# Hybrid encoder on one core: attention probabilities stored head-outermost, GpSimd writing the meta tokens' copies, and a weight split held behind the last merges

## The chip, the cores and the metric

The kernel runs as one program on one core of a Trainium2 chip. The metric is the device time of one execution in microseconds (us); the engines are PE (TensorE), DVE (VectorE), ACT (ScalarE), POOL (GpSimd) and SP (SyncE, which issues most DMAs). A matmul appears in the profile twice, as a weight load (PEld) and as the matmul itself (PE).

## The reference

Two encoder layers over 272 tokens (16 learned meta tokens and 256 real ones), 2048 channels, float32. Each layer:

```
h = rmsnorm(x);  q,k,v,f,ga,gf = h @ w_in
q,k = rope(rmsnorm(q)), rope(rmsnorm(k))
attn = softmax(q k^T / sqrt(128)) v          # 8 query heads, 2 kv heads
a = attn @ w_attn_br;  s = Re(fft2(f)) @ w_four
x = x + (sigmoid(ga)*a + sigmoid(gf)*s) @ w_out
x = x + (silu(dwconv3(rmsnorm(x) @ w_up_gate)) * (rmsnorm(x) @ w_up_val)) @ w_down
```

The meta tokens are dropped from the output, so the second layer computes its queries from token 14 on (`lo = 14`, 258 columns) where the first computes all 272 (`lo = 0`).

## The kernel before

Weights stream from HBM in chunks of 512 KB. Every chunk `raw` is split into a high part `wh` (ACT, line 303, a cast to fp32r) and a low part `wl` (DVE, line 306, the difference, two inputs in SBUF). A product is then three fp32r matmuls (lines 375 to 377): high by high, high by low, low by high. The activations stand split in the same way (`xH`/`xL`, `mH`/`mL`). Splits run up to three chunks ahead of PE (`LOOK = 3`); `split_w` issues them from a list, between pairs of matmuls.

Other work is put between the weight matmuls of the branch stage: a helper is a generator, each `yield n` waits for n pairs of matmuls, and `step()` advances it. The attention is such a generator. It runs beside the gate projections `ga` and `gf`, for one kv head (four query heads) at a time. Per kv head there are nine items: one for the meta tokens' queries of all heads, and for each of four heads two blocks of 128 queries. An item goes through

- `scores`: three matmuls into `ps_s`, maximum `mx` and bias `nb` on DVE, exponential on ACT (line 1079) into `pn`, one of four buffers of 128 queries by 384 columns; columns 112 to 383 hold the 272 probabilities, the meta tokens first; an ACT copy (line 1080) puts the 16 meta columns at 0, 32 and 64 too;
- `normalise`: reciprocal `rs` on DVE (line 1085), and one POOL instruction that scales all 384 columns of `pn` (line 1086);
- `transposed`, two items later: three PE transposes into `ps_pt`, then `PH`, the high part, on ACT (line 1106), `PL` and the meta rows' low part on DVE (lines 1107, 1109);
- `values`, for a head whose two blocks were transposed: seven matmuls into `ps_pv` (lines 1116 to 1119), three for each of two key blocks and one for the meta block.

`PH` is stored as (block, head, token) with 3 blocks and 4 heads, `PL` as (block, head, token) with 2. The program's order between engines is kept by semaphores that the framework sets from the regions that instructions read and write; it also orders each engine's instructions by a schedule of its own, except where code asks for the written order (`keep_in_program_order`).

At the end of each half of the branch stage come the merges: for each of the last channels, two DVE instructions make `th`, ACT casts `mH` (line 1227) and DVE makes `mL` (line 1228). The output projection `ps_o` (line 376 reads `mL`) follows at once.

Of the kernel before, what the change touches and what calls it, by code (L numbers as in the profile page):

```python
# [10 lines left out]
F32 = mybir.dt.float32  # L11
F32R = mybir.dt.float32r
AF = mybir.ActivationFunctionType
ALU = mybir.AluOpType
AX = mybir.AxisListType

P = 128
D = 2048
NM = 16
SEQ = 256  # L20
T = NM + SEQ
# [132 lines left out]
def _rep(ap, n):  # L154
    return ap.unsqueeze(1).to_broadcast([ap.shape[0], n, ap.shape[1]])
# [23 lines left out]
def encoder_kernel(ctx, tc, xT, params, consts, bmat, cfold, csign, w_fl, w_f64c, w_in, w_abr, w_four, w_f64, w_out, w_up, w_down, w_vn, w_dn, w_dt, out):  # L179
    nc = tc.nc  # L180
# [54 lines left out]
    t, done = 0, 0  # L235
# [61 lines left out]
    def split_w(i, a, b, parts="hl"):  # L297
        if i not in splits:
            splits[i] = split_tiles(i)
        h, lo = splits[i]  # L300
        r = raws[i]
        if "h" in parts:
            nc.scalar.copy(h[:, a:b], r[:, a:b])  # L303
        st["wl"] = lo
        if "l" in parts:
            nc.vector.tensor_tensor(lo[:, a:b], r[:, a:b], h[:, a:b].bitcast(F32), op=ALU.subtract)  # L306
            if b == CW:
                del raws[i]

# [301 lines left out]
    for l in range(DEPTH):  # L611
        last = l == DEPTH - 1
        lo = 14 if last else 0
# [4 lines left out]
        with tc.tile_pool(name=f"mix{l}", bufs=1) as mp:  # L618
# [429 lines left out]
            def attention(kv, rq):  # L1048
                qm = mp.tile([P, 2, 2, 4, NM], F32R, tag="qm", name="qm")
                for j, src in enumerate((qH, qL)):  # L1050
                    nc.scalar.copy(qm[:, j], src[kv][:, :, 0:NM].bitcast(F32).unsqueeze(1).to_broadcast([P, 2, 4, NM]))
                qmh, qml = (qm[:, j].rearrange("p r h t -> p (r h t)") for j in range(2))
                yield 3
                PHf = mp.tile([P, AHn], F32R, tag="aH", name="PH")
                PLf = mp.tile([P, ALn], F32R, tag="aL", name="PL")
                PH = PHf.rearrange("p (b h t) -> p b h t", b=3, h=4)
                PL = PLf.rearrange("p (b h t) -> p b h t", b=2, h=4)

                def scores(item):
                    if item is None:  # L1060
                        lh, ll, rcol = qmh, qml, rq[:, 8:9]
                    else:
                        h, i = item
                        c0, c1 = BLK[1 + i]
                        lh, ll = qH[kv][:, h, c0:c1], qL[kv][:, h, c0:c1]
                        rcol = rq[:, 2 * h + i:2 * h + i + 1]
                    ss = psum.tile([P, 512], F32, tag="aux", name="ps_s")
                    so = st2(ss[:, :T])
                    nc.tensor.matmul(so, lh, al(kH[:, kv, :]), start=True, stop=False)
                    nc.tensor.matmul(so, lh, al(kL[:, kv, :]), start=False, stop=False)  # L1070
                    nc.tensor.matmul(so, ll, al(kH[:, kv, :]), start=False, stop=True)
                    mx = small.tile([P, 1], F32, tag="mx", name="mx")
                    nc.vector.tensor_reduce(mx, ss[:, :T], axis=AX.X, op=ALU.max)
                    nb = small.tile([P, 1], F32, tag="nb", name="nb")
                    nc.vector.tensor_scalar(nb, mx, rcol, -1.0, op0=ALU.mult, op1=ALU.mult)
                    pn = pns[cnt[0] % 4]
                    cnt[0] += 1
                    sm = small.tile([P, 1], F32, tag="sm", name="sm")
                    nc.scalar.activation(hv(pn[:, P - NM:3 * P]), de(ss[:, :T]), AF.Exp, bias=nb, scale=rcol, accum_out=sm)
                    nc.scalar.copy(pn[:, 0:96].rearrange("p (a b) -> p a b", b=32)[:, :, 0:NM], _rep(pn[:, P - NM:P], 3))  # L1080
                    return pn, sm

                def normalise(pn, sm):
                    rs = small.tile([P, 1], F32, tag="rs", name="rs")
                    nc.vector.reciprocal(rs, sm)
                    nc.gpsimd.tensor_scalar(pn, pn, rs, None, op0=ALU.mult)
                    return pn

                def transposed(item, pn):
                    pt = psum.tile([P, 512], F32, tag="aux", name="ps_pt")  # L1090
                    for b in range(3):
                        s0 = (b + 1) % 3 * P
                        nc.tensor.transpose(pt[:, b * P:(b + 1) * P], pn[:, s0:s0 + P], ident)
                    if item is None:
                        src = pt[:, 0:3 * P].rearrange("p (b h t) -> p b h t", b=3, h=NH)[:, :, 0:4, :]
                        for b in range(3):
                            nc.scalar.copy(PH[:, b, :, 0:NM], src[:, b])
                        for b in range(2):
                            nc.vector.tensor_tensor(PL[:, b, :, 0:NM], src[:, b], PH[:, b, :, 0:NM].bitcast(F32), op=ALU.subtract)
                        x3 = PH[32:48, 2, :, 0:NM]  # L1100
                        nc.vector.tensor_tensor(x3, src[32:48, 2], x3.bitcast(F32), op=ALU.subtract)
                    else:
                        h, i = item
                        c0, c1 = BLK[1 + i]
                        src = pt[:, 0:3 * P].rearrange("p (b t) -> p b t", b=3)
                        nc.scalar.copy(PH[:, :, h, c0:c1], src)
                        nc.vector.tensor_tensor(PL[:, :, h, c0:c1], src[:, 0:2], PH[:, 0:2, h, c0:c1].bitcast(F32), op=ALU.subtract)
                        x3 = PH[32:48, 2, h, c0:c1]
                        nc.vector.tensor_tensor(x3, src[32:48, 2], x3.bitcast(F32), op=ALU.subtract)

                def values(h):
                    po = psum.tile([P, 512], F32, tag="aux", name="ps_pv")
                    vo = st2(po[:, :W])
                    for b in range(2):
                        ph, pl = al(PH[:, b, h, lo:T]), al(PL[:, b, h, lo:T])
                        nc.tensor.matmul(vo, VH[:, kv, b, :], ph, start=b == 0, stop=False)
                        nc.tensor.matmul(vo, VH[:, kv, b, :], pl, start=False, stop=False)
                        nc.tensor.matmul(vo, VL[:, kv, b, :], ph, start=False, stop=False)
                    nc.tensor.matmul(vo, V3[:, kv, :], al(PH[:, 2, h, lo:T]), start=False, stop=True)
                    nc.scalar.copy(hv(qH[kv][:, h, lo:T]), de(po[:, :W]))  # L1120
                    nc.vector.tensor_tensor(hv(qL[kv][:, h, lo:T]), de(po[:, :W]), hv(qH[kv][:, h, lo:T].bitcast(F32)), op=ALU.subtract)

                items = [None] + [(h, i) for h in range(4) for i in range(2)]
                lag, ready, due = [], [], []
                for item in items + ["end"] * 3:
                    if item != "end":
                        pe, sm = scores(item)
                    yield 2
                    if item != "end":
                        lag.append((item, normalise(pe, sm)))  # L1130
                    yield 1
                    done = lag.pop(0) if len(lag) == 3 or lag and item == "end" else None
                    if done is not None:
                        transposed(*done)
                        if done[0] is not None and done[0][1] == 1:
                            due.append(done[0][0])
                        yield 1
                    if ready:
                        values(ready.pop(0))
                    if done is not None:  # L1140
                        yield 1
                    ready, due = ready + due, []
                while ready:
                    values(ready.pop(0))
                    yield 1
# [43 lines left out]
            for half in range(2):  # L1189
                slow[2] = 0  # L1190
                mH = mL = None
                for n_, (kind, i) in enumerate(BRANCH_ORDER[half]):
# [21 lines left out]
                    else:  # L1214
# [7 lines left out]
                        for m in range(MG):  # L1222
                            k = 2 * j + m
                            t_, h_ = tha[i][:, m, lo:T], mH[:, k, lo:T]
                            nc.vector.scalar_tensor_tensor(hv(t_), hv(t_), 1.0, de(ps[m][:, :W]), op0=ALU.add, op1=ALU.mult)
                            nc.vector.tensor_tensor(t_, t_, thf[i][:, m, lo:T], op=ALU.add)
                            nc.scalar.copy(h_, t_)
                            nc.vector.tensor_tensor(mL[:, k, lo:T], t_, h_.bitcast(F32), op=ALU.subtract)  # L1228
                slow[2] = 22 if last else 20 if half else 15
                for mg in range(8):  # L1230
                    ps = group((l, "o", half, mg), lambda kt: (mH[:, kt, lo:T], mL[:, kt, lo:T]), W)
# [339 lines left out]
```

## Time and profile before

| what | value |
|---|---|
| median of 3 runs | 2376.45 us (2375.04 to 2378.63) |
| the profiled execution: time, span | 2377.1 us, 2375.2 us |
| PE busy | 2357.5 us (99%) |
| DVE busy | 1802.9 us (76%) |
| ACT busy | 1313.3 us (55%) |
| POOL busy | 191.5 us (8%) |
| attention of layer 0 and of layer 1 | about 125 to 220 us, 1345 to 1450 us |

The times are of the whole execution; the span runs from the first to the last instruction, 1.9 us less than the time. PE's busy time counts a matmul from its start to its modelled end, and neighbours overlap, so an idle gap in the list of waits is shorter than the time that PE lost there.

### The profile page before, as it was taken

Reading aid. Unit: us, or ns where it says so; the run is one execution under the profiler, and the core shown is the slowest. Engines: PE = TensorE matmul, PEld = TensorE weight load, DVE = VectorE, ACT = ScalarE, POOL = GpSimd, SP = SyncE. Lnnn points to the kernel's source line nnn. Section 1 sums busy time; section 2 is a strip of 40 time slices with the busy share of each in tenths; the row PEclk is TensorE's granted clock in tenths of the full one; section 3 lists DMA queues with packets and bytes.
Section 4 is the critical chain, followed back from the end, with each engine's and each line's share of the span. In section 5 each row is a group of like instructions: output and inputs, shape, how many; then the busy total and the mean of one; then the engine's idle time right before and its main releaser. Section 6 shows DMA issues by size and latency. Waiting matters only on the chain. (4 is left out here: it accounts for less than half of the span.)

```text
span 2375.2 us, 47690 instructions
## 1 busy us (share of the span) xinstructions
PE 2357.5 (99%) x18992; PEld 2305.7 (97%) x18992; DVE 1802.9 (76%) x2813; ACT 1313.3 (55%) x1929; POOL 191.5 (8%) x303
## 2 busy tenths in 40 slices
PE   9999999999999999999999999999999999999999
PEld 9999999999999999999999999999999999999998
DVE  7787867877777556767568877676888889888798
ACT  6565544554444334444455665445676666666575
POOL 0022110000000000000000131000010000000000
PEclk9999999999999999999999999999999999999999
DMA  7557999989999999999886546888889989988887
GB/s 268 178 165 229 305 297 318 294 285 337 319 316 309 320 325 328 309 322 310 263 261 202 182 151 217 263 287 256 285 303 307 323 291 307 306 305 282 258 283 264
DMA packets 171217, 660.70 MB, mean 278 GB/s; under 512 B 19425, under 2 KB 24673, under 8 KB 170097
## 3 DMA queue, kind: packets, MB, share of 16 engines
q1 hardware_dynamic: 152528, 538.07, 64.5%
q0 software_dynamic: 17024, 117.45, 19.7%
q8 instruction: 149, 2.44, 0.4%
q10 hardware_dynamic: 1440, 2.13, 0.3%
q14 instruction: 76, 0.61, 0.1%
HBM read 635.91 MB, written 136.31 MB: 325 GB/s over the span
## 5 line engine op out<-in xcount | busy, mean ns | idle before, releaser
L306 DVE TENSOR_TENSOR wl<-raw,wh 128x1024 fp32r<-128x1024 f32 (+1 forms) x937 | 1129.4, 1218 | 463.4 <-ACT wh L303 449.7
L303 ACT CAST wh<-raw 128x1024 fp32r<-128x1024 f32 (+1 forms) x937 | 966.3, 1041 | 717.2 <-PE ps_ug L376 192.3
L377 PE MATMUL ps_ug<-xHL,wl 128*128 128x272 f32 (+1 forms) x1408 | 390.3, 277 | 0.6 <-DVE wl L306 0.6
L375 PE MATMUL ps_ug<-xHL,wh 128*128 128x272 f32 (+1 forms) x1408 | 390.8, 278 | 0.0
L376 PE MATMUL ps_ug<-xHL,wh 128*128 128x272 f32 (+1 forms) x1408 | 390.0, 277 | 0.0
L376 PEld LDWEIGHTS ps_ug<-xHL,wh 128*128 128x128 f32 x1408 | 267.4, 190 | 2.1
L375 PEld LDWEIGHTS ps_ug<-xHL,wh 128*128 128x128 f32 x1408 | 267.4, 190 | 2.1
L377 PEld LDWEIGHTS ps_ug<-xHL,wl 128*128 128x128 f32 x1408 | 267.5, 190 | 1.0 <-DVE wl L306 1.0
L377 PE MATMUL ps_d<-gHL,wl 128*128 128x272 f32 x704 | 196.4, 279 | 0.0
L375 PE MATMUL ps_uv<-xHL,wh 128*128 128x272 f32 x704 | 196.4, 279 | 0.0
L376 PE MATMUL ps_d<-gHL,wh 128*128 128x272 f32 x704 | 196.4, 279 | 0.0
L376 PE MATMUL ps_uv<-xHL,wh 128*128 128x272 f32 x704 | 196.4, 279 | 0.0
L375 PE MATMUL ps_d<-gHL,wh 128*128 128x272 f32 x704 | 196.4, 279 | 0.0
L377 PE MATMUL ps_uv<-xHL,wl 128*128 128x272 f32 x704 | 196.4, 279 | 0.0
L1414 PE MATMUL ps_p<-wh,opnd 128*128 128x512 f32 x688 | 177.1, 380 | 0.0
L560 POOL COPY tick<-wl 128x1 f32<-128x1 f32 x112 | 38.1, 340 | 1501.7 <-DVE wl L306 1476.9
L371 PE MATMUL ps_uv<-xHL,wh 128*128 128x512 f32 x448 | 149.9, 382 | 0.0
L375 PE MATMUL ps_ga<-xHL,wh 128*128 128x272 f32 (+1 forms) x512 | 143.9, 281 | 0.0
L376 PE MATMUL ps_o<-mL,wh 128*128 128x272 f32 (+1 forms) x512 | 141.9, 277 | 1.4 <-DVE mL L1228 1.4
L375 PE MATMUL ps_gf<-xHL,wh 128*128 128x272 f32 (+1 forms) x512 | 143.2, 280 | 0.0
L376 PE MATMUL ps_gf<-xHL,wh 128*128 128x272 f32 (+1 forms) x512 | 141.8, 277 | 0.0
L377 PE MATMUL ps_gf<-xHL,wl 128*128 128x272 f32 (+1 forms) x512 | 141.8, 277 | 0.0
(371 smaller groups left out, 5989.9 us busy)
## 6 DMA issues: line engine op xcount, KB each, us to landing
raw<-in_w_up SPq DMA_DIRECT2D x320, 512.0 KB, 5.6
raw<-in_w_in SPq DMA_DIRECT2D x191, 512.0 KB, 4.4
raw<-in_w_down SPq DMA_DIRECT2D x88, 512.0 KB, 6.6
raw<-ft SPq DMA_DIRECT2D x80, 512.0 KB, 5.1
raw<-in_w_out SPq DMA_DIRECT2D x64, 512.0 KB, 6.1
ft<-in_w_dn POOLq DMA_DIRECT2D x30, 1024.0 KB, 12.1
raw<-in_w_dn SPq DMA_DIRECT2D x60, 512.0 KB, 5.0
raw<-in_w_abr SPq DMA_DIRECT2D x32, 512.0 KB, 4.8
```

Source lines behind the costliest of these rows:

```text
L303: nc.scalar.copy(h[:, a:b], r[:, a:b])
L306: nc.vector.tensor_tensor(lo[:, a:b], r[:, a:b], h[:, a:b].bitcast(F32), op=ALU.subtract)
L371: nc.tensor.matmul(o2, h[:, c, sl], ab, start=kt == 0, stop=False)
L375: nc.tensor.matmul(o, h[:, c, sl], a, start=kt == 0, stop=False)
L376: nc.tensor.matmul(o, h[:, c, sl], b, start=False, stop=False)
L377: nc.tensor.matmul(o, lo[:, c, sl], a, start=False, stop=kt == nk - 1)
L560: tc.keep_in_program_order(nc.gpsimd.tensor_copy(tick, st["wl"][:, 0, 0:1].bitcast(F32)))
L1414: nc.tensor.matmul(st2(ps[h]), x, al(w[:, 512 * h:512 * h + 512]), start=fresh and (s_, q) in BEGIN and first, stop=(s_, q) in END and end ...
```

## The change

Three edits. `PH` and `PL` are stored with the head outermost: (head, block, token). The ACT copy of line 1080 is gone; `normalise` issues two POOL instructions, one that scales the 16 meta columns into the three places 0, 32 and 64, and one that scales columns 112 to 383 in place. After the last merges of a half, the next split of a low weight part is kept behind what was issued before it.

```
 split_w:
-            nc.vector.tensor_tensor(lo[:, a:b], r[:, a:b], h[:, a:b].bitcast(F32), op=ALU.subtract)
+            sub = nc.vector.tensor_tensor(lo[:, a:b], r[:, a:b], h[:, a:b].bitcast(F32), op=ALU.subtract)
+            if st.pop("merged", False):
+                tc.keep_in_program_order(sub)
 attention:
-                PH = PHf.rearrange("p (b h t) -> p b h t", b=3, h=4)
-                PL = PLf.rearrange("p (b h t) -> p b h t", b=2, h=4)
+                PH = PHf.rearrange("p (h b t) -> p h b t", b=3, h=4)
+                PL = PLf.rearrange("p (h b t) -> p h b t", b=2, h=4)
 scores:
-                    nc.scalar.copy(pn[:, 0:96].rearrange("p (a b) -> p a b", b=32)[:, :, 0:NM], _rep(pn[:, P - NM:P], 3))
 normalise:
-                    nc.gpsimd.tensor_scalar(pn, pn, rs, None, op0=ALU.mult)
+                    nc.gpsimd.tensor_scalar(pn[:, 0:96].rearrange("p (a b) -> p a b", b=32)[:, :, 0:NM], _rep(pn[:, P - NM:P], 3), rs, None, op0=ALU.mult)
+                    nc.gpsimd.tensor_scalar(pn[:, P - NM:], pn[:, P - NM:], rs, None, op0=ALU.mult)
 values (and transposed in the same way):
-                        ph, pl = al(PH[:, b, h, lo:T]), al(PL[:, b, h, lo:T])
+                        ph, pl = al(PH[:, h, b, lo:T]), al(PL[:, h, b, lo:T])
 branch stage, after each "a" group's merges:
+                        st["merged"] = j == 3
```

On PE, in layer 1 and before the change, the third head of the first kv head. Names in brackets are the semaphores that an instruction waits for, by the engine that raises them.

```order
L1116 MATMUL ps_pv<-PH,VH 128x258 [waits DVE_49,Activation_49]
L1117 MATMUL ps_pv<-PL,VH 128x258 [waits DVE_49]
L1118 MATMUL ps_pv<-PH,VL 128x258
L1116 MATMUL ps_pv<-PH,VH 128x258 [waits Activation_49]
L375 MATMUL ps_ga_1_17858<-xHL,wh_17867 128x258
L376 MATMUL ps_ga_1_17858<-xHL,wh_17867 128x258
L377 MATMUL ps_ga_1_17858<-xHL,wl_17868 128x258
L375 MATMUL ps_ga_1_17858<-xHL,wh_17867 128x258
L1117 MATMUL ps_pv<-PL,VH 128x258 [waits DVE_49]
L1118 MATMUL ps_pv<-PH,VL 128x258
L1119 MATMUL ps_pv<-PH,V_82 128x258
```

The same head on PE with the change (the file is two lines longer here, so line 1116 is now 1118).

```order
L1118 MATMUL ps_pv<-PH,VH 128x258 [waits DVE_49,Activation_49]
L1119 MATMUL ps_pv<-PL,VH 128x258 [waits DVE_49]
L1120 MATMUL ps_pv<-PH,VL 128x258
L1118 MATMUL ps_pv<-PH,VH 128x258
L1119 MATMUL ps_pv<-PL,VH 128x258
L1120 MATMUL ps_pv<-PH,VL 128x258
L1121 MATMUL ps_pv<-PH,V_82 128x258 [waits DVE_49]
```

The second key block no longer waits for ACT and DVE, and the seven matmuls stand together. The semaphore counts that those two waits of before named belong to the `PH` and `PL` of the following head's first item. This is so for the first three heads of both kv heads in layer 1; in layer 0 the second block had no such waits before either, and PE's order there is unchanged.

On DVE, at the end of the second half of layer 0's branch stage, before the change (`XT` is the residual stream):

```order
L1225 SCALAR_TENSOR_TENSOR th<-th,ps_a_1_6094 128x272 [waits PE_49]
L1226 TENSOR_TENSOR th<-th 128x272 [waits DVE_49]
L306 TENSOR_TENSOR wl_6174<-raw_5985,wh_6173 128x1024 [waits DMAHW7_49,Activation_49]
L1228 TENSOR_TENSOR mL<-th,mH 128x272 [waits Activation_49] x2
L306 TENSOR_TENSOR wl_6204<-raw_6020,wh_6203 128x1024 [waits PE_49,DMAHW0_49,Activation_49,Pool_49]
L1235 SCALAR_TENSOR_TENSOR XT<-ps_o_0_0_6163,XT 128x272 [waits PE_49]
```

And with the change:

```order
L1227 SCALAR_TENSOR_TENSOR th<-th,ps_a_1_6094 128x272 [waits PE_49]
L1228 TENSOR_TENSOR th<-th 128x272 [waits DVE_49]
L1230 TENSOR_TENSOR mL<-th,mH 128x272 [waits Activation_49] x2
L306 TENSOR_TENSOR wl_6174<-raw_5985,wh_6173 128x1024 [waits DMAHW7_49]
L306 TENSOR_TENSOR wl_6204<-raw_6020,wh_6203 128x1024 [waits PE_49,DMAHW0_49,Activation_49,Pool_49]
L1238 SCALAR_TENSOR_TENSOR XT<-ps_o_0_0_6163,XT 128x272 [waits PE_49]
```

One split has moved behind the last two `mL`. The other three half ends show the same move.

On POOL, at the start of layer 1's attention, before the change (`rq` is the query norm's factor):

```order
L515 TENSOR_TENSOR rq<-qv,mhalf 128x9 [waits DVE_49]
L908 MEMSET qp 128x2x14 [waits DMAHW6_49,PE_49,Pool_49]
L909 MEMSET qps 128x2x14 [waits DMAHW5_49,DVE_49,PE_49]
L1086 TENSOR_SCALAR pn_16188<-pn_16188,rs 128x384 [waits DVE_49,Activation_49]
L1086 TENSOR_SCALAR pn_16189<-pn_16189,rs 128x384 [waits DVE_49,Activation_49]
```

And with the change:

```order
L517 TENSOR_TENSOR rq<-qv,mhalf 128x9 [waits DVE_49]
L910 MEMSET qp 128x2x14 [waits DMAHW6_49,PE_49,Pool_49]
L911 MEMSET qps 128x2x14 [waits DMAHW5_49,DVE_49,PE_49]
L1087 TENSOR_SCALAR pn_16188<-pn_16188,rs 128x3x16 [waits DVE_49]
L1088 TENSOR_SCALAR pn_16188<-pn_16188,rs 128x272 [waits Pool_49]
L1087 TENSOR_SCALAR pn_16189<-pn_16189,rs 128x3x16 [waits DVE_49]
L1088 TENSOR_SCALAR pn_16189<-pn_16189,rs 128x272 [waits Pool_49]
```

Each item has two POOL instructions, the first waiting for the reciprocal alone, the second for the first. ACT's 36 copies are gone from its queue; SP's queue is unchanged.

More of the change, by code (lines that the diff above doesn't have):

```diff
@@ L1096, in transposed @@
                         for b in range(3):
-                            nc.scalar.copy(PH[:, b, :, 0:NM], src[:, b])
+                            nc.scalar.copy(PH[:, :, b, 0:NM], src[:, b])
                         for b in range(2):
-                            nc.vector.tensor_tensor(PL[:, b, :, 0:NM], src[:, b], PH[:, b, :, 0:NM].bitcast(F32), op=ALU.subtract)
-                        x3 = PH[32:48, 2, :, 0:NM]
+                            nc.vector.tensor_tensor(PL[:, :, b, 0:NM], src[:, b], PH[:, :, b, 0:NM].bitcast(F32), op=ALU.subtract)
+                        x3 = PH[32:48, :, 2, 0:NM]
                         nc.vector.tensor_tensor(x3, src[32:48, 2], x3.bitcast(F32), op=ALU.subtract)
@@ L1105, in transposed @@
                         src = pt[:, 0:3 * P].rearrange("p (b t) -> p b t", b=3)
-                        nc.scalar.copy(PH[:, :, h, c0:c1], src)
-                        nc.vector.tensor_tensor(PL[:, :, h, c0:c1], src[:, 0:2], PH[:, 0:2, h, c0:c1].bitcast(F32), op=ALU.subtract)
-                        x3 = PH[32:48, 2, h, c0:c1]
+                        nc.scalar.copy(PH[:, h, :, c0:c1], src)
+                        nc.vector.tensor_tensor(PL[:, h, :, c0:c1], src[:, 0:2], PH[:, h, 0:2, c0:c1].bitcast(F32), op=ALU.subtract)
+                        x3 = PH[32:48, h, 2, c0:c1]
                         nc.vector.tensor_tensor(x3, src[32:48, 2], x3.bitcast(F32), op=ALU.subtract)
@@ L1118, in values @@
                         nc.tensor.matmul(vo, VL[:, kv, b, :], ph, start=False, stop=False)
-                    nc.tensor.matmul(vo, V3[:, kv, :], al(PH[:, 2, h, lo:T]), start=False, stop=True)
+                    nc.tensor.matmul(vo, V3[:, kv, :], al(PH[:, h, 2, lo:T]), start=False, stop=True)
                     nc.scalar.copy(hv(qH[kv][:, h, lo:T]), de(po[:, :W]))
```

## The prediction

> **What bounds the kernel now.** I read the page's busy shares first, then the list of PE's waits, then the two attention stages by windows, and last the timeline around each wait.
>
> ```profile
> span 2375.2 us, 47690 instructions
> PE 2357.5 (99%) x18992; PEld 2305.7 (97%) x18992; DVE 1802.9 (76%) x2813; ACT 1313.3 (55%) x1929; POOL 191.5 (8%) x303
> ```
>
> PE is busy 99%. The change removes no matmul, so it can win only what PE stands still. The waits of PE, all of them in the first fence and those of layer 1's attention (1365 to 1450 us) in the second; the columns are idle us, times, longest:
>
> ```profile
> PE ps_f L442 <- ACT wh L303: 5.1, 2, 4.5
> PE ps_f L845 <- DVE qp L913: 2.6, 1, 2.6
> PE ps_pv L1116 <- ACT PH L1106: 2.3, 4, 1.0
> PE ps_pv L1117 <- DVE PL L1107: 2.0, 4, 1.1
> PE ps_o L376 <- DVE mL L1228: 1.4, 1, 1.4
> PE ps_ug L377 <- DVE wl L306: 0.6, 2, 0.4
> ```
>
> ```profile
> PE ps_pv L1116 <- ACT PH L1106: 2.3, 4, 1.0
> PE ps_pv L1117 <- DVE PL L1107: 1.8, 3, 1.1
> ```
>
> The edits touch the third, fourth and fifth row: 2.3 + 2.0 + 1.4 = 5.7 us. Of that, 4.1 us lie in layer 1's attention, 0.2 in layer 0's, and 1.4 in one wait before an output projection. In those stages no other engine is full:
>
> ```profile
> 125.00:220.00 95.00, 94.77 (x822) 94.57 (x821) 73.48 (x158) 58.58 (x127) 30.23 (x25) 1.00 0.56 179
> 1345.00:1400.00 55.00, 53.05 (x464) 51.92 (x463) 43.30 (x92) 33.50 (x70) 15.86 (x10) 1.00 0.48 154
> 1400.00:1450.00 50.00, 47.80 (x419) 46.99 (x418) 37.21 (x82) 29.49 (x68) 14.80 (x9) 1.00 0.47 155
> ```
>
> After the width of the window come PE, PEld, DVE, ACT and POOL busy, then the granted clock (full) and DMA. Layer 0 loses 0.23 us of PE in 95, layer 1 loses 1.95 + 2.20 = 4.15 us in 105, with DVE at 43.30 + 37.21 = 80.5 us.
>
> **1. Head outermost.** One wait of each kind, on PE:
>
> ```profile
> 1369.75 0.28 PE L1117 MATMUL ps_pv<-PL,VH 128*128 128x258 f32 x1
> 1369.87 0.28 PE L1118 MATMUL ps_pv<-PH,VL 128*128 128x258 f32 x1
> 1371.15 0.38 PE L1116 MATMUL ps_pv<-PH,VH 128*128 128x258 f32 x1 [1.01 <-ACT PH L1106]
> 1371.36 0.28 PE L375 MATMUL ps_ga<-xHL,wh 128*128 128x258 f32 x1
> ...
> 1372.71 0.28 PE L375 MATMUL ps_ga<-xHL,wh 128*128 128x258 f32 x1
> 1373.51 0.38 PE L1117 MATMUL ps_pv<-PL,VH 128*128 128x258 f32 x1 [0.52 <-DVE PL L1107]
> ```
>
> ```profile
> 1370.63 0.47 ACT L1106 CAST PH<-ps_pt 128x384 fp32r<-128x384 f32 x1
> ```
>
> The first block's matmuls of this head ran; the second block's L1116 started 0.05 us after an ACT cast had written `PH` (1370.63 + 0.47 = 1371.10). By the order of the instructions that cast belongs to the next head. It writes nothing that this matmul reads: with the block outermost, a write of all blocks of one head spans the second block of its neighbour, and the semaphore follows the span. With the head outermost the order shows the second block without any wait, for three heads of each kv head. So I take all layer-1 waits of these two rows as gone.
>
> Their price is more than the idle column. Undisturbed, matmuls start 0.11 to 0.12 us apart (1369.75 to 1369.87) though each lasts 0.28. At the first wait the step is 1369.87 to 1371.15, 1.28 us, a loss of 1.17 where 1.01 is shown as idle: 0.16 more. The matmul after it comes 0.21 us later instead of 0.11 (1371.15 to 1371.36): 0.10 more. With 4 + 3 waits: 4.1 + 7 x 0.26 = 5.9 us. Shorter ones, under the idle column's reach because the running matmul covers them, add two or three tenths each, as here, where the second of these starts 0.46 us after the first though 0.21 was free:
>
> ```profile
> 1381.20 0.38 PE L1116 MATMUL ps_pv<-PH,VH 128*128 128x258 f32 x1 [0.17 <-ACT PH L1106]
> 1381.66 0.38 PE L1117 MATMUL ps_pv<-PL,VH 128*128 128x258 f32 x1
> ```
>
> I take 6.4 us; the ends are 4.1 (the idle alone) and 6.8.
>
> What is late next? The waits that stay are the true ones: a head's own `PH` and `PL`. For the head above they did not hold the first block back (0.28 us rows with no bracket). Three items between a transpose and its use remain. Weight splits follow PE, since their buffers come free by PE, and in the fence above no PE wait on `wl` or `wh` stands. DVE has 105 - 80.5 = 24.5 us of air against 6.4. Layer 0's one wait is at a last head, whose `PL` is its own, and it stays:
>
> ```profile
> 219.87 0.38 PE L1117 MATMUL ps_pv<-PL,VH 128*128 128x272 f32 x1 [0.23 <-DVE PL L1107]
> ```
>
> **2. The split behind the merges.** DVE, ACT and PE around the one wait:
>
> ```profile
> 454.35 0.44 DVE L1226 TENSOR_TENSOR th<-th 128x272 f32<-128x272 f32 x1
> 454.71 1.22 DVE L306 TENSOR_TENSOR wl<-raw,wh 128x1024 fp32r<-128x1024 f32 x1
> 455.84 0.79 DVE L1228 TENSOR_TENSOR mL<-th,mH 128x272 fp32r<-128x272 f32 x2
> ```
>
> ```profile
> 454.00 0.42 ACT L1227 CAST mH<-th 128x272 fp32r<-128x272 f32 x1 [1.67 <-DVE th L1226]
> 454.82 0.42 ACT L1227 CAST mH<-th 128x272 fp32r<-128x272 f32 x1 [0.40 <-DVE th L1226]
> ```
>
> ```profile
> 454.63 0.28 PE L375 MATMUL ps_o<-mH,wh 128*128 128x272 f32 x1
> 456.33 0.38 PE L376 MATMUL ps_o<-mL,wh 128*128 128x272 f32 x1 [1.42 <-DVE mL L1228]
> ```
>
> PE waits for the first of two `mL`, made after a split of 1.22 us. Without the split ahead, the first `mL` runs from 454.79, where `th` ends, to 455.23 (half of 0.79 plus overlap, taken as 0.44): PE goes on at 455.28 instead of 456.33, 1.05 us earlier. The second `mL` needs the second `mH`, done at 455.24, so it ends about 455.75; PE asks for it three matmuls later, at 455.63, and waits 0.15 us. Gain 0.9 us; ends 0.5 and 1.4. The split itself comes 0.9 us later. Splits are made up to three chunks of 24 matmuls ahead of PE (24 x 0.11 = 2.6 us each), so the delay lies in that lead. The three other half ends show no PE wait and give nothing.
>
> **3. GpSimd writes the copies.** 36 ACT copies of 0.23 us go (8.3 us of ACT, which nobody on the path waits for). POOL gets 36 pairs in place of 36 single instructions:
>
> ```profile
> L1080 ACT COPY pn<-pn x36: 217/231/248, 126.6 to 1435.8; 128x48 f32<-128x48 f32 x36
> L1086 POOL TENSOR_SCALAR pn<-pn,rs x36: 1237/1245/2332, 127.5 to 1436.2; 128x384 f32<-128x384 f32 x36
> ...
>   PEld ps_pt L1093: 0.2, 1
> ```
>
> ```profile
> L560 POOL COPY tick<-wl x112: 175/184/4247, 190.8 to 2070.1; 128x1 f32<-128x1 f32 x112
> ```
>
> The three numbers are min, median, max ns. From one column (184 ns) to 384 (1245 ns) POOL costs 2.77 ns a column: 314 ns for 48 columns and 935 for 272, together 1.25 us, the same as before. The pair starts without the ACT copy, and its second half adds a wait on the first. The lower end is two halves that overlap, 0.3 us less; the upper end follows from this:
>
> ```profile
> 182.04 1.23 DVE L306 TENSOR_TENSOR wl<-raw,wh 128x1024 fp32r<-128x1024 f32 x1 [0.77 <-ACT wh L303]
> ```
>
> ```profile
> 182.24 2.14 POOL L1086 TENSOR_SCALAR pn<-pn,rs 128x384 f32<-128x384 f32 x1 [1.10 <-ACT pn L1080]
> ```
>
> POOL's instruction lasted 2.14 us, not 1.24, where a split had begun 0.20 us before it; it ended 1.11 us after that split. So a running split holds POOL up, and between the halves of a pair DVE now has a place to begin one: at most 1.23 us more per pair. The Trainium skill, "SBUF — State Buffer", section "Who interferes with whom", says that a DVE instruction with two SBUF inputs and a GpSimd instruction that reads SBUF exclude each other, and that the one issued first keeps the ports for its whole length; the two rows agree, and by that rule alone each pair is open to one more lost turn.
>
> Who waits for POOL? The transposes, two items later. In the fence above only one weight load of 108 ever waited for `pn`, 0.2 us. It is the first item of layer 1, where PE lost 0.14 us (0.25 instead of 0.11):
>
> ```profile
> 1355.71 0.28 PE L377 MATMUL ps_ga<-xHL,wl 128*128 128x258 f32 x1
> 1355.96 0.55 PE L1093 MATMUL ps_pt<-cst,pn 128*128 128x128 f32 x3
> ```
>
> A lost turn there costs up to 1.2 us; POOL's earlier start by the copy's 0.23 us works against it. I charge 0.3, with ends -0.1 and 1.2. On POOL's queue the weight sums' ticks and DMA issues keep their places between the items, so they move with a pair by what it differs from 1.25 us, and no wait of PE in the first fence is for them.
>
> **The sum.** 6.4 + 0.9 - 0.3 = 7.0 us off the profiled execution's 2377.1: 2370.1. The median of the runs lies 0.65 lower, so 2369.5 us, 0.29% less. With all low ends the gain is 4.1 + 0.5 - 1.2 = 3.4 (2373.1); with all high ones 8.3 (2368.2). A change under 0.2%, 4.8 us, is about what a measurement of this kernel cannot tell from none.
>
> **Rivals.**
> *Half given back.* PE reaches its next needs 6 us sooner and finds some of them late: the next scores' bank, the transposes, a split on a DVE that makes the rope products in the same stretch. For it: before the second wait above DVE worked without a break. Against it: 24.5 us of DVE air, and buffers that follow PE. Half of 7.0 is left: 2373.0.
> *The waits stay.* If PE is held at these places by something that ended just before the cast, the layout changes nothing: only 0.9 us, 2375.5. Against it: the 0.05 us between the cast's end and the start, and the order.
> *POOL becomes late (slower).* PE never waited for 35 of 36 items, so there is room; the item at 1376.99 below was scaled 6.9 us before its transposes. If each pair took about 5 us instead of 1.25, the items with two to four us of room would hold PE in turn. To end slower than no change by 0.2% they must cost 7.3 + 4.8 = 12.1 us, 0.34 us on each of 36: 2382. The lost turns of 1.23 us are too short for that.
>
> ```profile
> 1376.99 1.25 POOL L1086 TENSOR_SCALAR pn<-pn,rs 128x384 f32<-128x384 f32 x1 [2.42 <-DVE rs L1085]
> ```
>
> ```profile
> 1385.12 0.49 PE L1093 MATMUL ps_pt<-cst,pn 128*128 128x128 f32 x3
> ```
>
> **How the numbers follow.** The sum's case 0.70 (2367 to 2372), half given back 0.20, the waits stay 0.06, POOL late 0.04. Faster by over 0.2% (under 2371.7): 0.66 of the first and 0.04 of the second case, 0.70. Slower by over 0.2%: 0.04. The rest, 0.26, within. The range 2367.0 to 2374.5 holds the first case and most of the second.
>
> **What would show it.** Right: in layer 1's attention the list of PE's waits has no L1118 or L1119 on `PH` or `PL` over 0.3 us, and PE's busy time there is within 0.5 us of the window; the wait for `mL` near 455 us is 0.3 to 0.6 us; POOL's two groups have medians near 0.31 and 0.94 us. Wrong: new waits of PE for `pn`, `ps_s` banks or `wl` between 1345 and 1450 us, or a second POOL half over 2 us in most items.

## The result, and the profile after

The changed kernel takes 2368.97 us (median of 15 runs, 2366.54 to 2374.43) against 2376.37 us for the kernel before in the same comparison (15 runs, 2373.05 to 2379.95): the ratio is 0.9973, with a 95% interval of 0.9966 to 0.9979. (The ratios here and below are those on record, over all runs of both kernels; the quotient of the two medians can differ from them by up to 0.0006.) 2369.5 was predicted, with a range of 2367.0 to 2374.5. The profiled execution took 2369.69 us. The page's first rows of the changed kernel:

```profile
span 2367.9 us, 47672 instructions
PE 2354.6 (99%) x18992; PEld 2304.4 (97%) x18992; DVE 1803.2 (76%) x2813; ACT 1306.8 (55%) x1893; POOL 190.7 (8%) x339
```

PE has the same 18992 matmuls, 7.3 us less span, of which 2.9 us were counted as busy and 4.4 us as idle. Busy time shrinks although the matmuls are the same, since a matmul after a wait is shown longer (0.38 against 0.28 us) and the matmuls around a wait overlap less (the 0.16 and 0.10 us that the prediction adds to the idle column). PE's waits in the changed kernel, as idle us, times and longest:

```profile
PE ps_f L444 <- ACT wh L303: 5.0, 2, 4.5
PE ps_f L847 <- DVE qp L915: 2.8, 1, 2.8
PE ps_uv L374 <- DVE wl L306: 0.4, 1, 0.4
PE ps_pt L1095 <- POOL pn L1088: 0.4, 1, 0.4
PE ps_pt L1095 <- ACT se L1207: 0.4, 1, 0.4
PE ps_ug L379 <- DVE wl L306: 0.3, 1, 0.3
PE ps_pv L1119 <- DVE PL L1109: 0.2, 1, 0.2
```

The waits for `PH` and `PL` are gone but for layer 0's one (0.2 us), and so is the wait for `mL`. Two short ones are new, both of the transposes `ps_pt`: one for POOL's scaled `pn`, one for ACT's copy `se`. The attention stages by windows of the changed kernel (width, PE, PEld, DVE, ACT, POOL, clock, DMA):

```profile
125.00:220.00 95.00, 94.77 (x822) 94.57 (x821) 74.60 (x158) 54.93 (x109) 29.70 (x43) 1.00 0.55 178
1345.00:1400.00 55.00, 54.57 (x489) 54.38 (x488) 44.50 (x95) 32.10 (x63) 18.65 (x21) 1.00 0.52 168
1400.00:1450.00 50.00, 49.59 (x443) 49.43 (x443) 37.83 (x82) 30.20 (x60) 11.96 (x16) 1.00 0.52 164
```

In layer 1, PE lacks 0.43 and 0.41 us where it lacked 1.95 and 2.20: exactly the two new waits. PE, and in the first window DVE, run more instructions in the same windows because work has moved forward in time. The third head of the first kv head, whose second block had waited 1.01 and 0.52 us, now on PE in the changed kernel:

```profile
1368.31 0.28 PE L1118 MATMUL ps_pv<-PH,VH 128*128 128x258 f32 x1
1368.42 0.28 PE L1119 MATMUL ps_pv<-PL,VH 128*128 128x258 f32 x1
1368.54 0.28 PE L1120 MATMUL ps_pv<-PH,VL 128*128 128x258 f32 x1
1368.65 0.28 PE L1118 MATMUL ps_pv<-PH,VH 128*128 128x258 f32 x1
1368.76 0.28 PE L1119 MATMUL ps_pv<-PL,VH 128*128 128x258 f32 x1
1368.87 0.28 PE L1120 MATMUL ps_pv<-PH,VL 128*128 128x258 f32 x1
1368.98 0.28 PE L1121 MATMUL ps_pv<-PH,V 128*128 128x258 f32 x1
```

Seven matmuls start 0.11 to 0.12 us apart, without a break.

Since both programs have the same number of matmuls on PE, the n-th can be set against the n-th: the difference of their starts, each from its span's start, is what PE has gained up to there. The steps of this difference are a ledger, and it is used for all kernels below (us, minus is earlier than before; the mark of a column is the time in the profile before):

| kernel | 450 to 460 (`mL`) | 1350 to 1357 (first `pn`) | 1357 to 1441 (value products) | 1441 to 1445 (bank) | all |
|---|---|---|---|---|---|
| changed kernel | -1.70 | +0.45 | -6.74 | +0.61 | -7.33 |
| layout alone | -0.39 | 0.00 | -6.74 | +0.53 | -5.21 |
| split behind the merges alone | -1.46 | -0.01 | -0.02 | 0.00 | -3.65 |
| GpSimd copies alone | -0.06 | +0.45 | +0.03 | 0.00 | +0.10 |
| layout and split | -0.86 | 0.00 | -6.74 | +0.53 | -8.86 |
| layout before, whole rows read | -1.15 | 0.00 | -6.54 | +0.49 | -6.70 |
| changed, POOL's pair turned (1st, 2nd time) | -0.66, -1.17 | -0.20, -0.20 | -6.73, -6.73 | +0.44, +0.45 | -9.18, -7.62 |
| before, once more | -0.17 | 0.00 | +0.03 | 0.00 | -1.04 |
| changed, once more | -1.69 | +0.45 | -6.74 | +0.60 | -6.65 |
| changed, POOL's work doubled | -1.69 | +2.33 | -6.74 | +0.83 | -4.67 |

What a row's steps do not hold lies at places that no edit touches: the first 50 us, where PE waits for the first weights, the wait for `qp` near 1285 us, and waits for single weight splits after 1750 us. Between two profiles of the very same program these places together differ by 0.7 us (changed kernel), 0.9 (kernel before) and 2.1 (turned pair), so the last column tells less than the others.

### The profile page after: what moved, and what is told of

Same layout as the page of the kernel before. It is cut to its first block, busy times and chain, and to the rows that moved or that the text cites. A ratio compares the mean times of both kernels' runs of the same rounds, so it can differ in the third digit from the quotient of the medians.

```text
span 2367.9 us, 47672 instructions
## 1 busy us (share of the span) xinstructions
PE 2354.6 (99%) x18992; PEld 2304.4 (97%) x18992; DVE 1803.2 (76%) x2813; ACT 1306.8 (55%) x1893; POOL 190.7 (8%) x339
## 5 line engine op out<-in xcount | busy, mean ns | idle before, releaser
L377 PE MATMUL ps_ga<-xHL,wh 128*128 128x272 f32 (+1 forms) x512 | 143.9, 281 | 0.0
L377 PE MATMUL ps_gf<-xHL,wh 128*128 128x272 f32 (+1 forms) x512 | 143.2, 280 | 0.0
L378 PE MATMUL ps_ga<-xHL,wh 128*128 128x272 f32 (+1 forms) x512 | 141.8, 277 | 0.0
L379 PE MATMUL ps_ga<-xHL,wl 128*128 128x272 f32 (+1 forms) x512 | 141.8, 277 | 0.0
```

The source lines that it names most:

```text
L377: nc.tensor.matmul(o, h[:, c, sl], a, start=kt == 0, stop=False)
L378: nc.tensor.matmul(o, h[:, c, sl], b, start=False, stop=False)
L379: nc.tensor.matmul(o, lo[:, c, sl], a, start=False, stop=kt == nk - 1)
```

## The experiments

**Each edit by itself.** Three kernels have one of the three edits each, a fourth has the first two and keeps ACT's copy.

Layout alone:

```
-                PH = PHf.rearrange("p (b h t) -> p b h t", b=3, h=4)
+                PH = PHf.rearrange("p (h b t) -> p h b t", b=3, h=4)
 (PL and all uses in the same way; split_w, scores and normalise as before)
```

> Only the layout of PH and PL is changed (head outermost); the ACT copy, the single POOL instruction and the order of the splits stay as before. Theory (the gain is the waits that the layout takes off PE in layer 1's attention): between the changed and the first kernel PE gained 6.6 us there, so 6.0 to 6.6 us less than before, a ratio of 0.9972 to 0.9975, and no wait of PE for PH or PL over 0.3 us between 1345 and 1450 us. Rival (the gain came from ACT's lighter queue and from the merges, and the waits only move): under 2 us, ratio above 0.999, with waits of PE for pn, for banks or for splits in the same stretch.

Measured: 2370.31 us (6 runs) against 2377.03 for the kernel before (22 runs), ratio 0.9969 (0.9958 to 0.9981). Its waits in the profile that lie at the places of the change:

```profile
PE ps_o L376 <- DVE mL L1228: 1.0, 1, 1.0
...
PE ps_pt L1093 <- ACT se L1205: 0.3, 1, 0.3
PE ps_pv L1117 <- DVE PL L1107: 0.2, 1, 0.2
```

All of layer 1's waits for `PH` and `PL` are gone with this edit alone, 6.74 us in the ledger, and 6.7 us in the medians, just over the 6.0 to 6.6 expected. The interval of the runs is 4.5 to 10 us, and the profiled execution alone is 5.2 us shorter, so the size is the ledger's and the medians only agree with it. The wait for the bank of `se` comes with it (and with each kernel that has this gain); the wait for `pn` doesn't.

Split behind the merges alone:

```
+            if st.pop("merged", False):
+                tc.keep_in_program_order(sub)
+                        st["merged"] = j == 3
```

> Only the split behind the last merges is changed. Theory A (the wait of 1.42 us before the output projection near 455 us stands in every execution): 0.9 to 1.6 us less than before, ratio about 0.9995, and the profile shows no wait of PE for mL, or one of under 0.6 us. Theory B (that wait came from a weight chunk that landed late in the one profiled execution of before, since DVE stood 1.34 us for a cast at 446 us there and 0.20 us in the changed kernel): no difference in time, and the profiles of kernels without this edit mostly show no such wait either. Both expect the seven waits in layer 1's attention to stay, about 4.1 us idle.

Measured: 2375.68 us (11 runs), ratio 0.9992 (0.9983 to 1.0001): 1.35 us less by the medians, which the runs do not tell from nothing. In its profile the wait for `mL` is gone, and the seven waits in layer 1 (one of the eight is layer 0's) are as before:

```profile
PE ps_pv L1118 <- ACT PH L1108: 2.3, 4, 1.0
PE ps_pv L1119 <- DVE PL L1109: 2.0, 4, 1.1
```

GpSimd copies alone:

```
-                    nc.scalar.copy(pn[:, 0:96]...[:, :, 0:NM], _rep(pn[:, P - NM:P], 3))
-                    nc.gpsimd.tensor_scalar(pn, pn, rs, None, op0=ALU.mult)
+                    nc.gpsimd.tensor_scalar(pn[:, 0:96]...[:, :, 0:NM], _rep(pn[:, P - NM:P], 3), rs, None, op0=ALU.mult)
+                    nc.gpsimd.tensor_scalar(pn[:, P - NM:], pn[:, P - NM:], rs, None, op0=ALU.mult)
```

> Only the meta copies are moved from ACT to GpSimd (two POOL instructions per item); the old layout and the old order of the splits stay. Theory (36 pairs of 1.37 us in place of 36 instructions of 1.24 us, of which only the first item of layer 1 lies on PE's path): 0.3 to 0.8 us slower than before, inside the measurement's spread, ratio 1.0000 to 1.0005; one wait of PE for pn of about 0.4 us at the first transposes of layer 1, and the waits for PH and PL as before. Rival (the lighter ACT queue makes PH earlier): the waits for PH in layer 1 shrink by 0.2 us each, 1 to 2 us in all, ratio about 0.9994.

Measured: 2377.32 us (11 runs), ratio 0.9999 (0.9990 to 1.0008). Its profile shows the new wait without either other edit:

```profile
PE ps_pt L1093 <- POOL pn L1086: 0.4, 1, 0.4
```

So this wait is the pair's doing, not a result of PE arriving sooner. The rival does not show: the waits for `PH` are 0.5 us shorter in this profile (1.8 us idle) and those for `PL` 0.3 us longer (2.3), and over the value products the ledger has +0.03.

Layout and split, with ACT's copy and POOL's single instruction:

> The changed kernel without its GpSimd part: head outermost and the split behind the merges, with the ACT copy and the single POOL instruction of before. Theory (the GpSimd part costs the wait of 0.43 us idle, 0.5 us of PE time, at the first transposes of layer 1): 0.3 to 0.6 us faster than the changed kernel, ratio to the first kernel 0.9966 to 0.9972, no wait for pn there. Rival (the freed ACT helps elsewhere): slower than the changed kernel by 0.5 us or more, with waits for PH or wh that the changed kernel does not have.

Measured: 2368.15 us (5 runs), ratio 0.9963 (0.9951 to 0.9976). No wait for `pn`; at the merges this is left:

```profile
PE ps_o L378 <- DVE mL L1230: 0.3, 1, 0.3
```

It is 0.8 us under the changed kernel by the medians, which were not taken side by side, and the two intervals overlap. The third edit, then, brings no gain that was seen, and costs a wait.

**Why the second block waited.** The prediction said that a write of all blocks of one head spans the second block of its neighbour. But layer 0 has the same writes in the same layout, and only the one wait for a head's own `PL`. What differs there is the read: 272 of 272 columns, not 258. A kernel with the layout of before was given whole-row reads in layer 1:

```
-                    vo = st2(po[:, :W])
+                    vo = st2(po[:, :T])
-                        ph, pl = al(PH[:, b, h, lo:T]), al(PL[:, b, h, lo:T])
+                        ph, pl = al(PH[:, b, h, 0:T]), al(PL[:, b, h, 0:T])
 (the read of block 2 and both evacuations in the same way)
```

> The kernel before, with the block outermost as it was and neither of the other edits; only layer 1's value products read whole rows of PH and PL (columns 0 to 271, not 14 to 271), and 14 more columns are evacuated. Theory: the false waits follow the region that a matmul is taken to read, and that is wider than its row only where it reads a part of the row (258 of 272 columns); layer 0, which reads whole rows, never had them. Then layer 1's attention (1345 to 1450 us) shows no PE wait for PH or PL of over 0.3 us, and the gain is that of the layout edit, 6.7 us, less 56 matmuls x 4 ns (112 to 116 ns apart) = 0.2 us: about 6.5 us under the kernel before, 2370.5. The wait for mL near 455 us stays, at 1.0 to 1.4 us. Rival: the block-outermost layout itself makes the waits, whatever part of a row is read (as the prediction put it, a write of all blocks spans the neighbour's second block); then the 7 waits of 4.1 us stay, and the time is that of before or 0.2 us more.

Measured: 2370.31 us (7 runs) against 2376.66 (16 runs), ratio 0.9973 (0.9962 to 0.9983). Its windows, and the only wait of PE from 1345 to 1450 us:

```profile
1345.00:1400.00 55.00, 55.00 (x492) 54.83 (x491) 45.09 (x96) 34.38 (x74) 15.86 (x10) 1.00 0.48 162
1400.00:1450.00 50.00, 49.71 (x444) 49.55 (x443) 38.03 (x83) 31.37 (x69) 13.89 (x9) 1.00 0.49 167
```

```profile
PE ps_pt L1093 <- ACT se L1205: 0.3, 1, 0.3
```

The waits are gone with the layout untouched, and the ledger has 6.54 us, the layout's 6.74 less the 0.2 us for 14 more columns. So the wait needs both: blocks outermost, and a read of part of a row. (This kernel also evacuates 14 more columns of `ps_pv`; those instructions neither read nor write `PH` or `PL`.) How the framework compares the two regions inside was not looked into; that it takes the partial read for wider than it is, is what these two kernels suggest, not what they show.

One line of this expectation failed: the wait for `mL` was to stay at 1.0 to 1.4 us, and was 0.27.

```profile
455.24 0.38 PE L376 MATMUL ps_o<-mL,wh 128*128 128x272 f32 x1 [0.27 <-DVE mL L1228]
```

This kernel has no split edit. Something else moves that wait.

**What moves the wait for `mL`.** ACT's casts of the weight chunks near 445 us, first in the kernel before, then in the whole-row kernel:

```profile
442.69 1.03 ACT L303 CAST wh<-raw 128x1024 fp32r<-128x1024 f32 x1
445.19 1.04 ACT L303 CAST wh<-raw 128x1024 fp32r<-128x1024 f32 x1 [1.04 <-DMA raw<-in_w_out]
```

```profile
442.75 1.03 ACT L303 CAST wh<-raw 128x1024 fp32r<-128x1024 f32 x1
444.11 1.03 ACT L303 CAST wh<-raw 128x1024 fp32r<-128x1024 f32 x1
```

In the first ACT waits 1.04 us for a chunk of `in_w_out`; in the second the chunk is there. DVE's split needs the cast. It is in the kernel before, then in the whole-row kernel:

```profile
446.32 1.23 DVE L306 TENSOR_TENSOR wl<-raw,wh 128x1024 fp32r<-128x1024 f32 x1 [1.34 <-ACT wh L303]
```

```profile
445.23 1.23 DVE L306 TENSOR_TENSOR wl<-raw,wh 128x1024 fp32r<-128x1024 f32 x1 [0.19 <-ACT wh L303]
```

In the first DVE is 1.09 us later, and at the merges the two waits for `mL` differ by 1.15 us. The bracket of the cast, beside the ledger's step at 450 to 460 us, for all profiles (us):

| no split edit | chunk late | step | split edit | chunk late | step |
|---|---|---|---|---|---|
| before | 1.04 | 0 | turned pair, 1st | 1.15 | -0.66 |
| GpSimd copies alone | 0.99 | -0.06 | layout and split | 0.92 | -0.86 |
| before, once more | 0.89 | -0.17 | turned pair, 2nd | 0.78 | -1.17 |
| layout alone | 0.65 | -0.39 | split alone | 0.50 | -1.46 |
| whole rows | 0 | -1.15 | changed, both times; doubled | 0 | -1.70, -1.69; -1.69 |

In each half of the table the step follows the chunk, about 1 us of it for 1 us. Between the halves, at equal lateness, lie 0.55 us (chunk in time) to about 0.9 (0.65 late); at the 1.04 of the kernel before, between the first two rows on the right, 0.76 - 0 = 0.76. That is what the edit is worth. The rest of the 1.70 in the profile of the changed kernel goes with the chunk's arrival. Of the two theories for the split alone, each is right in part. The chunk sets most of the wait, as theory B had it, but four of the five profiles without the edit show a wait of 1.0 to 1.4 us, where B expected mostly none; and the edit is worth 0.55 us or more at every lateness, as A had it. At the three other half ends the ledger shows no step. The kernel before was profiled once more to see whether the chunk is always late there:

> The kernel before, unchanged, profiled once more. Theory: the mL wait near 455 us is the split's 1.2 us only in part; the rest is chance, namely whether a chunk of in_w_out lands 1 us late at about 445 us (ACT's cast of it then waits for the DMA, DVE's split for the cast). With the chunk late the wait is 1.0 to 1.4 us as before, with the chunk in time 0.3 us as in the whole-row kernel. Rival: the split alone makes it, and it is 1.0 to 1.4 us either way. The seven waits in layer 1's attention recur, 3.5 to 4.5 us.

Measured: 2376.03 us in one run, with the chunk 0.89 us late and this wait; layer 1's waits recur at 2.3 and 1.7 us:

```profile
455.53 0.38 PE L376 MATMUL ps_o<-mL,wh 128*128 128x272 f32 x1 [1.25 <-DVE mL L1228]
```

It agrees with the theory's late case; whether the chunk can be in time in exactly this program was not seen. Nor is it shown that the arrival is chance. Each of the three programs that were profiled twice had the chunk nearly alike both times (1.04 and 0.89 us late, in time twice, 1.15 and 0.78 late), and the changed kernel with POOL's work doubled, described below, had it in time too. That the arrival belongs to the program, the changed kernel's among them, stays open.

**The pair on POOL.** In the changed kernel POOL, DVE and PE at the first items of layer 1:

```profile
1351.44 1.85 POOL L1087 TENSOR_SCALAR pn<-pn,rs 128x48 f32<-128x48 f32 x1 [20.70 <-DVE rs L1086]
1353.38 1.20 POOL L1088 TENSOR_SCALAR pn<-pn,rs 128x272 f32<-128x272 f32 x1
```

```profile
1351.25 0.71 DVE L933 TENSOR_TENSOR qp<-qp,cst 128x544 f32<-128x544 f32 x1
1351.87 1.22 DVE L306 TENSOR_TENSOR wl<-raw,wh 128x1024 fp32r<-128x1024 f32 x1
```

```profile
1354.63 0.55 PE L1095 MATMUL ps_pt<-cst,pn 128*128 128x128 f32 x3 [0.43 <-POOL pn L1088]
```

The 48-column instruction took 1.85 us instead of 0.40: it ended 0.20 us after the split. The 272-column one, which the transposes need first (they read columns 128 to 383 before 0 to 127), stands behind it and ends at 1354.58, 0.05 us before PE starts. The Trainium skill, "SBUF — State Buffer", section "Who interferes with whom", says that a DVE instruction with two SBUF inputs and a GpSimd instruction that reads SBUF exclude each other. The rows agree: POOL's instruction was held through the two DVE products above, which lasted until 1353.09. That it was held through the second too, which began 0.43 us after it, is what these rows show; the section's rule, by which the one issued first has the ports, would not have said so. In the turned pair the long half goes first, and a plain copy of the scaled columns follows:

```
-                    nc.gpsimd.tensor_scalar(pn[:, 0:96]...[:, :, 0:NM], _rep(pn[:, P - NM:P], 3), rs, None, op0=ALU.mult)
                     nc.gpsimd.tensor_scalar(pn[:, P - NM:], pn[:, P - NM:], rs, None, op0=ALU.mult)
+                    nc.gpsimd.tensor_copy(pn[:, 0:96]...[:, :, 0:NM], _rep(pn[:, P - NM:P], 3))
```

> The changed kernel with POOL's pair turned round: columns 112 to 383 are scaled first, then a plain copy puts the 16 scaled columns at 0, 32 and 64. The first two transposes of an item read columns 128 to 383 alone. Theory: the 0.43 us wait of the first transposes of layer 1 comes from the 48-column instruction standing ahead of the one that they need; without it that wait is gone (PE 0.5 us earlier by 1356 us), the time 0.5 us under the changed kernel, 2368.5. A later item's third transpose may wait at most 0.1 us for the copy. Rival: DVE's split, which held the first of the pair for 1.4 us (1851 against 402 ns), holds whichever instruction comes first, and the 272-column one ends as late as before: the wait stays at 0.2 to 0.5 us and the time at 2369.0.

Measured: 2367.94 us (5 runs) against 2376.66, ratio 0.9963 (0.9951 to 0.9976). Its first pair on POOL, and the two groups:

```profile
1351.18 2.41 POOL L1087 TENSOR_SCALAR pn<-pn,rs 128x272 f32<-128x272 f32 x1 [20.70 <-DVE rs L1086]
1353.66 0.23 POOL L1088 COPY pn<-pn 128x48 f32<-128x48 f32 x1
```

```profile
L1087 POOL TENSOR_SCALAR pn<-pn,rs x36: 957/963/2413, 126.5 to 1428.9; 128x272 f32<-128x272 f32 x36
L1088 POOL COPY pn<-pn x36: 222/226/1166, 127.6 to 1430.0; 128x48 f32<-128x48 f32 x36
```

The instruction was held as before (2413 ns), so the rival was right about the hold, but nothing stood ahead of the instruction: the needed columns are ready at 1353.59, 1.0 us sooner, and the wait for `pn` is gone (-0.20 instead of +0.45 in the ledger). The copy also costs 226 ns where the scaling of the same columns costs 402.

The turned pair and the changed kernel once more, side by side on one chip:

> The changed kernel, unchanged, timed and profiled once more beside the turned pair. Theory: the waits for POOL's pn (0.3 to 0.5 us) and for the bank of se (0.3 to 0.6 us) recur, no mL wait over 0.4 us with either chunk, and the time is 2368 to 2370. Rival: the 0.4 us wait for pn was chance and is gone.

> The kernel with POOL's pair turned round, beside the changed kernel on the same chip. Theory: no wait for pn again, PE 0.5 us earlier at 1356 us, and 0.5 to 1 us less than the changed kernel, at the edge of what the runs can tell. Rival: no difference, both within 0.3 us.

Measured: the changed kernel 2370.41 us (11 runs), ratio 0.9976 (0.9967 to 0.9985) to the kernel before at 2375.87 (15 runs); the turned pair 2369.51 us (5 runs), ratio 0.9968 (0.9956 to 0.9981). The time of the changed kernel is above the 2368 to 2370 that was expected, that of the turned pair 0.9 us below it. In the profiles the waits recur as forecast: 0.4 for `pn` and 0.4 for `se` in the changed kernel, none for `pn` in the turned one. By the medians the turned pair is about 1 us ahead here, and also in the first pair of timings, which were not taken side by side; neither difference is clear of the intervals. 0.65 us of it is shown by the ledger, more is not.

**Whether POOL can become late.** To see the room behind POOL, its work for each item was doubled by two products by 1.0 behind the pair of the changed kernel:

```
+                    nc.gpsimd.tensor_scalar(pn[:, P - NM:], pn[:, P - NM:], 1.0, None, op0=ALU.mult)
+                    nc.gpsimd.tensor_scalar(pn[:, P - NM:P + 32], pn[:, P - NM:P + 32], 1.0, None, op0=ALU.mult)
```

> The changed kernel with two more POOL instructions behind each pair, a product by 1.0 over 272 and over 48 columns: POOL's work for an item doubles, 1.37 us more on each of 36. Theory: the items wait two turns for their transposes, so POOL's room is over 2 us for all but the first item of layer 1, which has none: PE loses 1.4 to 2.5 us there, in one or two waits for pn, and no other; 2370.4 to 2371.5, with layer 0 unchanged. Rival (POOL late, the slower case of the prediction): each item holds PE by 0.34 us or more, 12 us and up: 2381 or more, with waits for pn at most items of both layers.

Measured: 2373.18 us (10 runs) against 2376.66, ratio 0.9980 (0.9971 to 0.9990). All its waits of the transposes, and layer 0's window:

```profile
PE ps_pt L1097 <- POOL pn L1090: 2.3, 1, 2.3
...
PE ps_pt L1097 <- ACT se L1209: 0.6, 1, 0.6
```

```profile
125.00:220.00 95.00, 95.00 (x825) 94.99 (x824) 73.97 (x159) 55.09 (x109) 64.23 (x77) 1.00 0.52 179
```

POOL's busy time in layer 0 went from 29.70 to 64.23 us in 95, and PE lost nothing. Only the first item of layer 1 waits, 1.9 us more than in the changed kernel, within the 1.4 to 2.5 expected. The time is 1.7 us above what was expected. Against the profile of the changed kernel, this one loses another 0.8 us at the first weights and 1.5 us at two splits near 1845 us, 0.2 us at the bank near 1435 us, and gains 1.7 us at other places that no edit touches. The kernel with the layout alone waits at the same splits, so I do not put them down to POOL, but it isn't settled.

## Why the prediction was right, point by point

**Head outermost.** 6.4 us were forecast (4.1 to 6.8); the ledger has 6.74 in every kernel with this layout. Pricing a wait at its idle column plus 0.26 us was right: set against the kernel with the layout alone, the seven waits that the list shows hold 5.8 us, where 5.9 was worked out. Shorter ones, which the list does not show, hold the other 0.9, where the forecast allowed 0.5. The reason was half right. The false wait follows a region, but the span of the write alone doesn't make it, since whole-row reads in the same layout have none.

**Half given back.** This rival was the likeliest loss, and it was small: 0.5 to 0.6 us at one place, which the sum did not have. PE comes to the transposes near 1435 us while the bank that they need is still being copied out on ACT:

```profile
1435.17 0.28 ACT L1207 COPY se<-ps_s 128x138 f32<-128x138 f32 x1 [0.87 <-DVE sp L1211]
```

```profile
1435.55 0.52 PE L1095 MATMUL ps_pt<-cst,pn 128*128 128x128 f32 x3 [0.41 <-ACT se L1207]
```

ACT's copy had itself waited 0.87 us for DVE (`sp`), and DVE reached that late, behind two weight splits:

```profile
1431.43 2.36 DVE L306 TENSOR_TENSOR wl<-raw,wh 128x1024 fp32r<-128x1024 f32 x2 [0.23 <-ACT wh L303]
1434.79 0.29 DVE L1211 TENSOR_TENSOR sp<-se,so 128x134 f32<-128x134 f32 x1
```

So the rival's mechanism, a bank and a split on DVE that come late, was there, and the prediction's argument against it, DVE's 24.5 us of air over the two windows, did not hold at this place; but it cost 0.6 of 6.7 us, not half. "The waits stay" fell with the first profile. "POOL becomes late" needed about 5 us for a pair; a pair takes 1.365 us, and even doubled work held PE at one item alone.

**The split behind the merges.** Forecast 0.9 us (0.5 to 1.4), with 0.3 to 0.6 us of waiting left. At the chunk's arrival of the profile before it is 0.76, and 0.33 us of waiting is left in the kernel with layout and split, which is the forecast's picture. The changed kernel itself showed a step of 1.70 and no wait, outside the ends: the forecast took the wait for one that the split alone makes, though a late DMA made about 1 us of it.

**The pair on POOL.** Charged at 0.3 us (-0.1 to 1.2); it was 0.45, all of it at the first item of layer 1, the place that the forecast named. The pair's own cost was sized too low:

```profile
L1087 POOL TENSOR_SCALAR pn<-pn,rs x36: 397/402/1851, 127.2 to 1430.0; 128x48 f32<-128x48 f32 x36
L1088 POOL TENSOR_SCALAR pn<-pn,rs x36: 962/963/2004, 127.7 to 1430.5; 128x272 f32<-128x272 f32 x36
```

1.365 us instead of 1.25. The step that failed is the line from a one-column copy (184 ns) to the 384-column product: these are two operations. The three products, 402, 963 and 1245 ns, lie on a line of 2.5 ns a column from about 280 ns; copies lie on another, 184 ns for one column and 226 for 48. The charge for lost turns was of the right kind, but they became fewer: counted in the timeline, 12 of 36 instructions took over 1.9 us before, and of 72 now 8 are 0.2 to 1.5 us longer than their median. The rule of that section of the Trainium skill left a second lost turn open to each pair; here the first pair of layer 1 shows one whole turn and a short one (1.85 us, then 1.20 instead of 0.96), and PE noticed no other.

**The sum.** -6.4 - 0.9 + 0.3 = -7.0 was forecast for the profiled execution, and -7.4 measured (2377.1 to 2369.69). The ledger: -6.74 + 0.61 - 1.70 + 0.45 = -7.38, and the places that no edit touches cancel to +0.05. So the agreement to 0.4 us is in part luck: it hides two misses of 0.8 and 0.6 with opposite signs, the chunk that was in time and the bank. On the second timing, 2370.41 against 2375.87, the gain was 5.5 us, and the time is still in the range.

**The signs.** Of the signs of being right, the waits for `PH` and `PL` are gone as forecast, and PE's busy time is within 0.5 us of both windows. The wait for `mL` was to be 0.3 to 0.6 us and is gone, and POOL's first group has a median of 0.40 us, not 0.31 (the second has 0.96, near 0.94). Of the signs of being wrong, one came in part: there are new waits of PE for `pn` and for a `ps_pt` bank between 1345 and 1450 us, one each of 0.4 us. No second POOL half was over 2 us but one (2.004).

## What to carry to other kernels

A wait in the profile has a price on PE (here idle plus 0.26 us each) and a releaser, and where the releaser writes nothing that the waiting matmul reads, one can look for the region that the framework saw: a partial read of a row in an interleaved tile was enough here, and either another layout or a whole-row read removed it. Before a wait is charged to the instruction that stands ahead of it, the releaser's own wait should be followed back one or two steps, to see whether a DMA that is late in some profiles and in time in others has a share. Where one instruction is cut in two, the part that is needed first goes first, and a part that can be a copy is a copy.

## What the runs showed that was not expected

POOL's copy of 48 columns took 226 ns, the product of the same columns with a per-partition factor 402. A product with the constant 1.0 was about 70 ns shorter than one with `rs`, by the shortest of each: 889 against 962 ns for 272 columns, 329 against 397 for 48:

```profile
L1089 POOL TENSOR_SCALAR pn<-pn x36: 889/1260/1981, 129.5 to 1433.7; 128x272 f32<-128x272 f32 x36
L1090 POOL TENSOR_SCALAR pn<-pn x36: 329/333/1335, 130.5 to 1435.6; 128x48 f32<-128x48 f32 x36
```

Since the 48 columns were contiguous with 1.0 and spread over three places with `rs`, and both sizes differ by the same, the spread form costs nothing that can be seen.
